# A decoder layer with every product turned to activations stationary, and its residual stream kept with tokens on the partitions

## The chip, the cores and the metric

The kernel runs on one core of one Trainium2 chip. The metric is the device time of one execution in microseconds (us). Names of engines: PE is TensorE (products and transposes), PEld its weight loads, DVE is VectorE, ACT is ScalarE, POOL is GpSimd, and SP's queue issues most DMAs.

## What is computed

One layer: two gated feed-forward blocks (SwiGLU) around a mixer of stick-breaking attention and a short convolution, each behind an RMS norm whose result is scaled and shifted by vectors (adaLN) that come from `c` through a 2048 x 18432 matrix. 256 tokens, width 2048, feed-forward width 5632, all float32.

```python
def swiglu(h, w_gu, w_down):
    gate, up = jnp.split(h @ w_gu, 2, axis=-1)
    return (jax.nn.silu(gate) * up) @ w_down
...
    mod = c_act @ w_ada[l] + b_ada[l]
    (sh1, sc1, g1, sh2, sc2, g2, sh3, sc3, g3) = jnp.split(mod, N_MOD, axis=-1)
    h = modulate(rms_norm(x), sh1, sc1)          # h * (1 + scale) + shift
    x = x + FFN_RES * g1[:, None, :] * swiglu(h, w1_gu[l], w1_down[l])
    h = modulate(rms_norm(x), sh2, sc2)
    x = x + g2[:, None, :] * hybrid_mixer(h, w_in[l], q_norm_w[l], k_norm_w[l], conv_w[l], w_out[l])
    h = modulate(rms_norm(x), sh3, sc3)
    x = x + FFN_RES * g3[:, None, :] * swiglu(h, w2_gu[l], w2_down[l])
```

In the mixer half of the width is attention (8 heads of 128), half is `gate_b * causal_short_conv(gate_c * u, conv_w)` with three taps along the tokens.

## The kernel before

**Weights and precision.** Each weight tile is 512 rows by 512 columns, one DMA of 1 MB on SP's queue into `raw` (five buffers). It is used in two halves of 256 rows. For each half ACT rounds the weights to the PE's fast float format (`high`, L358: `hi`) and DVE makes the rest (`prepare`, L364: `lo`). Activations are held the same way, as a pair of parts: `hS` for a normalised block, `act` and `mix` (tiles named `big`) for the inputs of the down and out products. A product is hi x hi + hi x lo + lo x hi.

**Two forms of product.** In `mm_N` (L477 to L486) the activations are stationary: for each of two groups of 128 tokens and each of two row blocks there are three products that stream 512 weight columns; the result has tokens on the partitions. In `mm_T` (L391) the weights are stationary: for each of four column blocks and two row blocks one product streams both parts of the activations (512 columns, L401) and one streams the high part (256 columns, L403); the result has channels on the partitions. `mm_D` (L406) splits the 512-column product in two of 256, used for the last column pair of a section. `mm_N` serves the gate and up columns and q, k, v; `mm_T` serves the down products, the convolution's c, u, b and the out products.

**Order of work.** `run` walks a list of entries written out by hand. For each half it emits `prepare`, then consumes the half that was prepared four halves earlier (AHEAD = 4): its products, and then `tick`, which emits work that was put off by a number of halves (`at`). In the last tile of a group the products of one pair of column blocks are held back (`held`) and follow in the last half, so the other pair finishes early. Each engine takes its instructions in the order in which they are emitted. Between weight tiles stand adaLN tiles (`ada_half`): DVE multiplies and adds them (L169), a block transpose and a sum fold them, and after some ticks (QP) one product of PE and four additions of DVE finish a section (L195, L203, L286).

**The start.** The first norm's scale and shift come in eight chunks of 256 channels (`ada_chunk`), mixed with weight tiles in eight windows (`windows`): two row blocks of `hS` become ready at each chunk's `end`, and column groups are visited several times, their partial sums being saved (L797) and loaded again (L776) by ACT. At a chunk's end all but two prepared halves are consumed (`keep`), then eight one-column products (`on_pe`, L233) finish the sums.

**The residual stream.** `xT` has channels on the partitions. x arrives with tokens on the partitions and is turned by 32 transposes (L598). `residual` copies the accumulator to `ev` on ACT (L463) and adds it on DVE with the gate as a value per partition (L638). The norm sums squares over partitions by products with ones (L672 to L677) and scales on DVE (L552); `norm_end` and `norm_rest` run in the gap between two sections (`fresh` in `run`). At the end `store` turns the result back (L842) and sends it from SP's queue.

Of the kernel before, what the change touches and what calls it, by code (L numbers as in the profile page):

```python
# [39 lines left out]
DB, DQ, DS, DL, DT = 1, 1, 0, 0, 0  # L40
OUT = 3
# [12 lines left out]
class Kern:  # L54
    def __init__(self, ctx, tc, x, c, w_ada, b_ada, w1_gu, w1_down, w_in, q_norm_w, k_norm_w,
                 conv_w, w_out, w2_gu, w2_down, out):
        self.tc, self.nc = tc, tc.nc
        self.x, self.c, self.out = x[0], c, out[0]
# [11 lines left out]
        self.ev = pool("ev", 2)  # L70
# [7 lines left out]
        self.have = set()  # L78

# [91 lines left out]
    def ada_half(self, sec, half):  # L171
# [25 lines left out]
        def finish():  # L197
            ps = st["ps"][:, 0:32].rearrange("p (j q) -> p q j", q=4)
            cs = slice(16 * sec + 8 * half, 16 * sec + 8 * half + 8)
            o, b = self.mod[:, cs], (self.b_lo[:, cs] if sec < 8 else self.b_hi[:, 8 * half:8 * half + 8])  # L200
            for q in range(4):
                r = slice(32 * q, 32 * q + 32)
                nc.vector.tensor_add(o[r], ps[r, q, :], b[r])  # L203
            self.ada_post(o, ("", "scale", "" if sec == 5 else "half")[sec % 3])
            self.have.add((sec, half))
# [19 lines left out]
    def ada_chunk(self, ch):  # L225
# [34 lines left out]
        def end():  # L260
            while self.soft:
                self.soft.popleft()()
# [7 lines left out]
            self.shifted(a, self.scaled(a))  # L270

        return ents, end

# [43 lines left out]
    def run(self, entries):  # L317
# [22 lines left out]
        for e in entries:  # L340
# [52 lines left out]
    def mm_T(self, accs, hi, lo, rhs, first, last, pairs=(0, 1)):  # L393

        nc = self.nc
        for pr in pairs:
            for i in range(2):
                for kk in range(2):
                    cs = slice((2 * pr + i) * P, (2 * pr + i + 1) * P)
                    o = accs[pr][i]  # L400
                    nc.tensor.matmul(o, hi[:, kk, cs], rhs[kk].rearrange("p a t -> p (a t)"),  # L401
                                     start=first and kk == 0, stop=False)
                    nc.tensor.matmul(o[:, 0:T], lo[:, kk, cs], rhs[kk][:, 0, :],  # L403
                                     start=False, stop=last and kk == 1)

    def mm_D(self, acc, hi, lo, rhs, first, last, i):  # L406

        nc = self.nc
        cs = slice((2 + i) * P, (3 + i) * P)
        o = acc[i][:, 0:T]  # L410
        for kk in range(2):
            nc.tensor.matmul(o, hi[:, kk, cs], rhs[kk][:, 0, :], start=first and kk == 0, stop=False)  # L412
            nc.tensor.matmul(o, hi[:, kk, cs], rhs[kk][:, 1, :], start=False, stop=False)  # L413
            nc.tensor.matmul(o, lo[:, kk, cs], rhs[kk][:, 0, :], start=False, stop=last and kk == 1)  # L414

    def group_T(self, w, rows, c0, rhs_of, finish, finish_one=None):
# [7 lines left out]
        def make(u):  # L424
            def cons(h, hi, lo):
                first, last = u == 0 and h == 0, u == nu - 1 and h == 1
                rhs = [rhs_of(4 * u + 2 * h + kk) for kk in range(2)]
                if first:
                    state["accs"] = [self.acc(), self.acc()]
                accs = state["accs"]  # L430
                if u < nu - 1 and finish_one:
                    self.mm_T(accs, hi, lo, rhs, first, False, (0,))
                    for i in range(2):
                        self.mm_D(accs[1], hi, lo, rhs, first, False, i)
                elif u < nu - 1:
                    self.mm_T(accs, hi, lo, rhs, first, False)
                elif h == 0:
                    self.mm_T(accs, hi, lo, rhs, first, False, (0,))
                    state["held"] = (accs, hi, lo, rhs, first, False, (1,))
                else:  # L440
                    self.mm_T(accs, hi, lo, rhs, False, True, (0,))
                    finish(0, accs[0])
                    if finish_one:
                        for i in range(2):
                            self.mm_D(accs[1], *state["held"][1:-1], i)
                            self.mm_D(accs[1], hi, lo, rhs, False, True, i)
                        for i in range(2):
                            finish_one(i, accs[1][i][:, 0:T])
                    else:
                        self.mm_T(*state["held"])  # L450
                        self.mm_T(accs, hi, lo, rhs, False, True, (1,))
                        finish(1, accs[1])
            return cons
# [5 lines left out]
    def evacuate(self, acc):  # L459

        c = self.ev.tile([P, 2, 512], F32, tag="ev", name=self.nm("ev"))
        for i in range(2):
            self.nc.scalar.copy(c[:, i, :], acc[i])  # L463
        return c

    def half_sum(self, acc, out):

        c = self.evacuate(acc)
        self.nc.vector.tensor_add(out, c[:, :, 0:T], c[:, :, T:2 * T])

    def split(self, dst, src):

        nc = self.nc
        nc.scalar.copy(dst[:, :, 0, :], src)  # L474
        nc.vector.tensor_sub(dst[:, :, 1, :], src, dst[:, :, 0, :].bitcast(F32))  # L475

    def mm_N(self, acc, hi, lo, h, first, last):  # L477

        nc = self.nc
        for tt in range(2):  # L480
            ts = slice(tt * P, (tt + 1) * P)
            for kk in range(2):
                nc.tensor.matmul(acc[tt], h[kk][:, 0, ts], hi[:, kk, :], start=first and kk == 0, stop=False, skip_group_check=True)  # L483
                nc.tensor.matmul(acc[tt], h[kk][:, 0, ts], lo[:, kk, :], start=False, stop=False, skip_group_check=True)  # L484
                nc.tensor.matmul(acc[tt], h[kk][:, 1, ts], hi[:, kk, :], start=False, stop=last and kk == 1,  # L485
                                 skip_group_check=True)  # L486

    def flip_split(self, dst, src):

        nc = self.nc  # L490
        for pr in range(2):
            ps = self.misc()
            for i in range(2):
                for tt in range(2):
                    nc.tensor.transpose(ps[:, i * T + tt * P:i * T + (tt + 1) * P],  # L495
                                        src[tt][:, (2 * pr + i) * P:(2 * pr + i + 1) * P], self.ident)
            self.split(dst[:, 2 * pr:2 * pr + 2], ps.rearrange("p (i t) -> p i t", i=2))
# [19 lines left out]
    def norm_end(self, sec):  # L517

        self.rrow = self.ssq
# [3 lines left out]
        s, y = self.tmp(), self.rrow  # L523
        v, t = s[:, 0:T], s[:, T:2 * T]
        nc.scalar.activation(y, self.ss[:, 0:T], AF.Ln, bias=self.epsb, scale=1.0 / D)
        nc.scalar.activation(y, y, AF.Exp, scale=-0.5)
        nc.scalar.activation(t, y, AF.Square)

        def norm_rest():
            for u in (sec, sec + 1):  # L530
                self.want(u, 0)
            nc.vector.tensor_scalar(v, self.ss[:, 0:T], 1.0 / D, EPS, op0=ALU.mult, op1=ALU.add)
            xn = self.tmp()[:, 0:512].rearrange("p (i t) -> p i t", i=2)
            sc = self.mod[:, 16 * (sec + 1):16 * (sec + 1) + 2]
            nc.vector.scalar_tensor_tensor(xn[:, 0, :], self.xT[:, 0, :], sc[:, 0:1], y, op0=ALU.mult, op1=ALU.mult)
            nc.vector.scalar_tensor_tensor(t, t, -0.5, v, op0=ALU.mult, op1=ALU.mult)
            nc.vector.scalar_tensor_tensor(xn[:, 0, :], t, 1.5, xn[:, 0, :], op0=ALU.add, op1=ALU.mult)
            nc.vector.scalar_tensor_tensor(y, t, 1.5, y, op0=ALU.add, op1=ALU.mult)
            nc.vector.scalar_tensor_tensor(xn[:, 1, :], self.xT[:, 1, :], sc[:, 1:2], y, op0=ALU.mult, op1=ALU.mult)
            self.shifted(0, xn)  # L540
            self.h_done = 2
            self.prepare(1)
            self.need_h(4)
        self.norm_rest = norm_rest

    def scaled(self, k):

        nc = self.nc
        xn = self.tmp()[:, 0:512].rearrange("p (i t) -> p i t", i=2)
        for i in range(2):  # L550
            sc = self.mod[:, 16 * (self.h_sec + 1) + k + i:16 * (self.h_sec + 1) + k + i + 1]
            nc.vector.scalar_tensor_tensor(xn[:, i, :], self.xT[:, k + i, :], sc, self.rrow, op0=ALU.mult, op1=ALU.mult)  # L552
        return xn

    def shifted(self, k, xn):

        nc = self.nc
# [571 lines left out]
```

## Time and profile before

| | before |
|---|---|
| median of 3 runs | 1926.17 us (1925.99 to 1926.94) |
| the profiled execution | 1926.24 us, span 1924.5 us |
| PE busy | 1894.2 us, 98% of the span |
| DVE busy | 1416.2 us, 74% |
| ACT busy | 941.1 us, 49% |
| DMA | 500.78 MB, mean 260 GB/s |

The profile is one execution. Busy time is what the recorded instructions cover; products of PE overlap in it, since their ends are modelled, so the distance between starts, not the duration, is what one of them costs. The granted clock is the share of full speed that PE was given; its two levels are 1.2 and 2.4 GHz (0.5 and 1.0). The chain is followed back from the last instruction to what released each step.

### The profile page before, as it was taken

To read this page: it belongs to the slowest core of one execution; us is meant where nothing else is said; L and a number is where in the kernel's file an instruction comes from. 1 tells how busy PE (TensorE), PEld (TensorE's weight loads), DVE (VectorE), ACT (ScalarE), POOL (GpSimd) and SP (SyncE) were. 2 spreads that over 40 slices of the span, in tenths; PEclk is the share of its full clock that TensorE was granted. 3 is DMA by queue.
4 is the path that set the end of the run, shared out by engine and by line. 5 is a ranking of instruction groups with operands and counts; after the bars stand their busy time and mean duration, and the time that the engine had idled before them with its cause. 6 is when DMAs were issued, how large, how long until landed. Compare 5 with 4: busy or idle time off the path is not lost.

```text
span 1924.5 us, 24141 instructions
## 1 busy us (share of the span) xinstructions
PE 1894.2 (98%) x9517; PEld 1606.1 (83%) x9517; DVE 1416.2 (74%) x1652; ACT 941.1 (49%) x1195; POOL 2.0 (0%) x11
## 2 busy tenths in 40 slices
PE   5999999999999999999999999999999999999999
PEld 4888888888888888788888887888888888888888
DVE  7878888788787889788889997667675554445454
ACT  4667784444444444466554554544444444444443
POOL 0000000000000000000000000000000000000000
PEclk8999999999999999999999999999999999999999
DMA  9898988888888878677869885678875555555551
GB/s 365 307 331 299 339 289 305 304 289 317 303 307 310 309 281 309 217 253 272 284 229 333 297 307 191 206 256 282 279 269 189 192 186 197 186 187 196 183 193 63
DMA packets 240361, 500.78 MB, mean 260 GB/s; under 512 B 8382, under 2 KB 43384, under 8 KB 239992
## 3 DMA queue, kind: packets, MB, share of 16 engines
q1 hardware_dynamic: 240216, 499.24, 74.0%
q8 instruction: 74, 1.21, 0.2%
q14 instruction: 39, 0.32, 0.0%
q10 hardware_dynamic: 32, 0.01, 0.0%
HBM read 497.12 MB, written 2.10 MB: 259 GB/s over the span
## 4 chain that ended last, share of the span: by engine, by line
PE 97%; DVE 2%; DMA 1%; ACT 0%; issue 0%; SPq 0%; DVEq 0%
PE acc L401 23%; PE acc L483 19%; PE acc L484 19%; PE acc L485 19%; PE acc L403 12%; DVE ada L169 1%; PE m L495 1%; PE acc L413 1%; PE acc L414 1%; DMA raw<-in_w_ada_dram 1%; PE acc L412 1%; DVE lo L364 0%; PE m L233 0%; PE m L1015 0%; PE m L992 0%
## 5 line engine op out<-in xcount | busy, mean ns | idle before, releaser
L364 DVE TENSOR_TENSOR lo<-raw,hi 128x1024 fp32r<-128x1024 f32 x656 | 792.7, 1223 | 392.4 <-ACT hi L358 389.5
L358 ACT CAST hi<-raw 128x1024 fp32r<-128x1024 f32 x656 | 685.9, 1053 | 737.4 <-PE acc L485 373.9
L483 PE MATMUL acc<-hi,hS 128*128 128x512 f32 x1600 | 632.1, 395 | 7.9 <-ACT hS L560 7.2
L484 PE MATMUL acc<-lo,hS 128*128 128x512 f32 x1600 | 627.7, 392 | 1.3 <-DVE lo L364 1.3
L485 PE MATMUL acc<-hi,hS 128*128 128x512 f32 x1600 | 627.4, 392 | 0.0
L401 PE MATMUL acc<-big,hi 128*128 128x512 f32 x1552 | 548.9, 398 | 0.0
L403 PE MATMUL acc<-big,lo 128*128 128x256 f32 x1552 | 436.4, 281 | 0.0
L169 DVE SCALAR_TENSOR_TENSOR ada<-raw,cact,ada 128x1024 f32<-128x1024 f32 (+1 forms) x327 | 357.2, 1092 | 8.3 <-DMA raw<-in_w_ada_dram 1.3
L483 PEld LDWEIGHTS acc<-hi,hS 128*128 128x128 f32 x1600 | 303.1, 189 | 70.7 <-ACT hS L560 8.1
L484 PEld LDWEIGHTS acc<-lo,hS 128*128 128x128 f32 x1600 | 303.0, 189 | 63.8 <-DVE lo L364 2.3
L485 PEld LDWEIGHTS acc<-hi,hS 128*128 128x128 f32 x1600 | 302.8, 189 | 64.0 <-DVE hS L563 0.6
L401 PEld LDWEIGHTS acc<-big,hi 128*128 128x128 f32 x1552 | 291.7, 188 | 68.3
L403 PEld LDWEIGHTS acc<-big,lo 128*128 128x128 f32 x1552 | 293.9, 189 | 0.2
L401 PE MATMUL acc<-hS,hi 128*128 128x512 f32 x384 | 136.5, 400 | 0.0
L403 PE MATMUL acc<-hS,lo 128*128 128x256 f32 x384 | 107.5, 280 | 0.0
L401 PEld LDWEIGHTS acc<-hS,hi 128*128 128x128 f32 x384 | 72.2, 188 | 16.8
L638 DVE SCALAR_TENSOR_TENSOR xT<-ev,mod,xT 128x256 f32<-128x256 f32 x148 | 60.9, 480 | 21.0 <-ACT ev L463 20.9
L403 PEld LDWEIGHTS acc<-hS,lo 128*128 128x128 f32 x384 | 72.5, 189 | 0.0
L463 ACT COPY ev<-acc 128x512 f32<-128x512 f32 x98 | 50.6, 593 | 29.6 <-PE acc L403 29.2
L797 ACT COPY big<-acc 128x512 f32<-128x512 f32 x72 | 41.0, 587 | 37.2 <-PE acc L485 37.2
L475 DVE TENSOR_TENSOR big<-m,big 128x512 fp32r<-128x512 f32 x44 | 28.4, 686 | 22.2 <-ACT big L474 22.1
L560 ACT ACTIVATE hS<-t,mod 128x256 fp32r<-128x256 f32 x48 | 22.0, 503 | 41.6 <-DVE t L552 39.0
(141 smaller groups left out, 710.6 us busy)
## 6 DMA issues: line engine op xcount, KB each, us to landing
raw<-in_w_gu_dram SPq DMA_DIRECT2D x170, 1024.0 KB, 5.4
raw<-in_w_ada_dram SPq DMA_DIRECT2D x112, 1024.0 KB, 5.1
raw<-in_w_down_dram SPq DMA_DIRECT2D x88, 1024.0 KB, 5.7
raw<-in_w_in_dram SPq DMA_DIRECT2D x48, 1024.0 KB, 6.4
raw<-in_w_ada_dram SPq DMA_DIRECT2D x64, 512.0 KB, 6.2
raw<-in_w_out_dram SPq DMA_DIRECT2D x16, 1024.0 KB, 6.4
raw<-in_w_gu_dram SPq DMA_DIRECT2D x12, 512.0 KB, 6.0
big<-in_x_dram SPq DMA_DIRECT2D x2, 1024.0 KB, 7.1
```

Source lines behind the costliest of these rows:

```text
L169: nc.vector.scalar_tensor_tensor(acc, w, self.cact[:, k:k + 1], acc, op0=ALU.mult, op1=ALU.add)
L358: nc.scalar.copy(hi, raw[:, 2 * h:2 * h + 2, :])
L364: nc.vector.tensor_sub(lo, raw[:, 2 * h:2 * h + 2, :], hi.bitcast(F32))
L401: nc.tensor.matmul(o, hi[:, kk, cs], rhs[kk].rearrange("p a t -> p (a t)"), start=first and kk == 0, stop=False)
L403: nc.tensor.matmul(o[:, 0:T], lo[:, kk, cs], rhs[kk][:, 0, :], start=False, stop=last and kk == 1)
L463: self.nc.scalar.copy(c[:, i, :], acc[i])
L475: nc.vector.tensor_sub(dst[:, :, 1, :], src, dst[:, :, 0, :].bitcast(F32))
L483: nc.tensor.matmul(acc[tt], h[kk][:, 0, ts], hi[:, kk, :], start=first and kk == 0, stop=False, skip_group_check=True)
L484: nc.tensor.matmul(acc[tt], h[kk][:, 0, ts], lo[:, kk, :], start=False, stop=False, skip_group_check=True)
L485: nc.tensor.matmul(acc[tt], h[kk][:, 1, ts], hi[:, kk, :], start=False, stop=last and kk == 1, skip_group_check=True)
L638: self.nc.vector.scalar_tensor_tensor(xd, src, self.mod[:, 16 * gate + d:16 * gate + d + 1], xd, op0=ALU.mult, op1=ALU.add)
L797: nc.scalar.copy(slot(n)[:, pr, :], acc[pr])
```

## The change

All products take the form of `mm_N`: `mm_T`, `mm_D` and `group_T` go, and `group_N` also serves down, c, u, b and out. x stays with tokens on the partitions (`x`, two tiles), so the residual adds along the free axis, with the gate as a row that is the same on all partitions: `gate_row` turns the gate's columns by one transpose, writes them to DRAM and reads them back broadcast, both on POOL's queue. The squares are summed along the free axis by ACT. A block is normalised in place of tokens (ACT, a factor per partition), turned by PE (`flip`) into PSUM, and scaled, shifted and split by DVE and ACT (`modulated`). The convolution's c x u and b are turned by `flip` too. The result is stored from `x` with no transposes. The `fresh` break in `run` goes, so tiles of the next section are prepared across the norm. In the list of adaLN sections (6, 0) and (7, 0) move ahead of (5, 0) and (5, 1). Cut to its core:

```diff
         def end():
+            xn = self.normed(CB * ch)
             while self.soft:
                 self.soft.popleft()()
...
-            self.shifted(a, self.scaled(a))
+            self.modulated(a, xn)
...
+    def gate_row(self, sec, half, cols):
+        nc = self.nc
+        ps = self.misc()
+        nc.tensor.transpose(ps[0:8, 0:P], cols, self.ident)
+        row = self.small.tile([8, P], F32, tag="row", name=self.nm("row"))
+        nc.scalar.copy(row, ps[0:8, 0:P])
+        flat = self.dram.tile([8, P], F32, tag="flat", name=self.nm("flat"))
+        nc.gpsimd.dma_start(flat, row)
+        g = self.gatep.tile([P, 1024], F32, tag="gate", name=self.nm("gate"))
+        nc.gpsimd.dma_start(g, flat.rearrange("j p -> (j p)").partition_broadcast(P))
+        self.gates[sec, half] = g
...
-            if e.get("fresh"):
-                self.high, self.prepare = high, prepare
-                while pend and pend[0][0] is not e["cons"]:
-                    consume()
-                self.norm_rest()
-                continue
...
+    def group_N(self, w, rows, c0, lhs_of, finish, lead=False):
...
             def cons(h, hi, lo):
+                k = 4 * u + 2 * h
+                first, last = k == 0, u == nu - 1
+                if lead:
+                    self.need_h(k + 2)
                 if first:
+                    state["acc"] = self.acc()
+                acc = state["acc"]
+                lhs = [lhs_of(k + kk) for kk in range(2)]
+                if not last:
+                    self.mm_N(acc, hi, lo, lhs, first, False)
                 elif h == 0:
+                    self.mm_N(acc, hi, lo, lhs, first, False, (0,))
+                    state["held"] = (hi, lo, lhs, first, False, (1,))
                 else:
+                    self.mm_N(acc, hi, lo, lhs, False, True, (0,))
+                    self.mm_N(acc, *state["held"])
+                    self.mm_N(acc, hi, lo, lhs, False, True, (1,))
+                if lead:
+                    self.need_h(k + 6)
+                if last and h == 1:
+                    finish(acc)
...
+    def normed(self, k):
+        xn = self.tmp()
+        for tt in range(2):
+            self.nc.scalar.activation(xn[:, tt * T:(tt + 1) * T], self.x[tt][:, k * P:(k + 2) * P], AF.Copy,
+                                      scale=self.r[:, tt:tt + 1])
+        return self.flip([xn[:, tt * T:(tt + 1) * T] for tt in range(2)])[0]
+
+    def modulated(self, k, xn):
+        nc = self.nc
+        h = self.tmp()[:, 0:512].rearrange("p (i t) -> p i t", i=2)
         for i in range(2):
+            sh, sc = (self.mod[:, 16 * sec + k + i:16 * sec + k + i + 1] for sec in (self.h_sec, self.h_sec + 1))
+            nc.vector.tensor_scalar(h[:, i, :], xn[:, i, :], sc, sh, op0=ALU.mult, op1=ALU.add)
+        nc.scalar.copy(self.hS[:, k:k + 2, 0, :], h)
+        nc.vector.tensor_sub(self.hS[:, k:k + 2, 1, :], h, self.hS[:, k:k + 2, 0, :].bitcast(F32))
...
+    def residual(self, dg, acc, gate):
+        nc = self.nc
+        self.want(gate, dg // 2)
+        g = self.gates[gate, dg // 2][:, 512 * (dg % 2):512 * (dg % 2 + 1)]
+        for tt in range(2):
+            t = self.tmp()[:, 0:512]
+            nc.vector.tensor_mul(t, acc[tt], g)
+            xd = self.x[tt][:, 512 * dg:512 * (dg + 1)]
+            nc.vector.tensor_add(xd, xd, t)
+
+    def squares(self, dg, next_sec):
...
+        for tt in range(2):
+            sq = self.tmp()[:, 0:512]
+            nc.scalar.activation(sq, self.x[tt][:, 512 * dg:512 * (dg + 1)], AF.Square,
+                                 accum_out=self.parts[:, tt, dg:dg + 1])
+        if dg == 3:
+            self.rms(self.parts)()
+            self.norm_begin(next_sec)
...
+    def store(self, dg):
+        for tt in range(2):
+            cs = slice(512 * dg, 512 * (dg + 1))
+            self.nc.sync.dma_start(self.out[tt * P:(tt + 1) * P, cs], self.x[tt][:, cs])
```

In the convolution `fin_u` multiplies the accumulator by c on DVE, and two ticks later flips the product; three passes of DVE per 128 channels then read it from PSUM. `fin_b` copies b on ACT and flips it two ticks later.

## Rows read from the trace of the kernel before

**Rows 1.** The page: busy us, share, instructions; the chain by engine.
```profile
PE 1894.2 (98%) x9517; PEld 1606.1 (83%) x9517; DVE 1416.2 (74%) x1652; ACT 941.1 (49%) x1195; POOL 2.0 (0%) x11
...
PE 97%; DVE 2%; DMA 1%; ACT 0%; issue 0%; SPq 0%; DVEq 0%
```

**Rows 2.** Stretches: us, busy us (count) per engine, granted clock, DMA share, GB/s.
```profile
100.00:150.00 50.00, 50.00 (x230) 41.64 (x229) 40.37 (x54) 35.54 (x54) 0.00 (x0) 1.00 0.87 311
```

**Rows 3.** Groups by line and shape: count, busy us, mean ns, idle before.
```profile
L401 PE MATMUL acc<-big,hi 128*128 128x512 f32 x1552 | 548.9, 398 | 0.0
...
L401 PE MATMUL acc<-hS,hi 128*128 128x512 f32 x384 | 136.5, 400 | 0.0
...
L412 PE MATMUL acc<-big,hi 128*128 128x256 f32 x112 | 31.7, 283 | 0.0
```

**Rows 4.** Chain in order of time (start, us, what), activations stationary, 32 pieces.
```profile
1649.97 0.23 PE acc L484
...
1657.00 0.23 PE acc L485
```

**Rows 5.** The same chain with weights stationary, 41 pieces.
```profile
1849.92 0.12 PE acc L403
...
1856.99 0.12 PE acc L403
```

**Rows 6.** The same chain: sums at the chunk ends (first, last of six), eight transposes.
```profile
78.56 0.79 PE m L233 x8
...
235.64 0.79 PE m L233 x8
258.36 0.87 PE m L495 x8
```

**Rows 7.** Timeline of ACT at the third chunk's end: start, us, line, idle before.
```profile
112.19 0.58 ACT L797 COPY big<-acc 128x512 f32<-128x512 f32 x1 [0.77 <-PE acc L485]
112.67 1.11 ACT L776 COPY acc<-big 128x512 f32<-128x512 f32 x2
```

**Rows 8.** Groups by line and shape, for durations of DVE and ACT.
```profile
L701 DVE TENSOR_TENSOR t<-acc,t 128x512 f32<-128x512 f32 x44 | 28.3, 684 | 0.2
...
L474 ACT CAST big<-m 128x512 fp32r<-128x512 f32 x44 | 23.7, 590 | 37.6 <-PE m L495 37.6
...
L846 DVE COPY t<-m 128x256 f32<-128x256 f32 x8 | 3.4, 425 | 6.5 <-PE m L842 6.5
...
L844 ACT COPY t<-m 128x256 f32<-128x256 f32 x8 | 3.0, 372 | 15.2 <-PE m L842 15.2
```

**Rows 9.** Timeline of the first norm: small operations of ACT and DVE.
```profile
14.77 0.28 ACT L503 ACTIVATE nr<-nt,epsb 128x2 f32<-128x2 f32 x1
...
17.46 0.16 DVE L507 TENSOR_SCALAR nt<-nt 128x2 f32<-128x2 f32 x1
```

**Rows 10.** Timeline of PE: a short stop, and the first boundary between sections.
```profile
37.64 0.50 PE L483 MATMUL acc<-hi,hS 128*128 128x512 f32 x1 [0.66 <-ACT big L797]
...
786.12 0.59 PE L672 MATMUL m<-ssq,ones 128*128 128x256 f32 x2
...
791.36 0.56 PE L483 MATMUL acc<-hi,hS 128*128 128x512 f32 x1 [2.92 <-ACT hS L560]
```

**Rows 11.** Stretches behind both boundaries and around the short stop.
```profile
791.36:796.00 4.64, 4.64 (x13) 3.48 (x14) 3.83 (x8) 2.65 (x5) 0.00 (x0) 0.63 0.15 15
1178.15:1185.00 6.85, 6.85 (x18) 5.38 (x19) 5.59 (x10) 4.87 (x7) 0.00 (x0) 0.56 0.39 124
36.00:42.00 6.00, 5.34 (x24) 4.09 (x23) 5.75 (x9) 5.01 (x8) 0.00 (x0) 1.00 1.07 392
```

**Rows 12.** Timeline of DVE and ACT where a gate's section is finished.
```profile
397.50 1.22 DVE L364 TENSOR_TENSOR lo<-raw,hi 128x1024 fp32r<-128x1024 f32 x1
...
397.84 1.05 ACT L358 CAST hi<-raw 128x1024 fp32r<-128x1024 f32 x1 [1.99 <-PE acc L401]
...
399.47 0.17 DVE L286 TENSOR_SCALAR mod<-mod 128x8 f32<-128x8 f32 x1
```

More of the change, by code (lines that the diff above doesn't have):

```diff
@@ L78, in __init__ @@
         self.have = set()
+        self.gates = {}
     def nm(self, s):
@@ L390, in run, with split, mm_N @@
         self.flush()
-    def mm_T(self, accs, hi, lo, rhs, first, last, pairs=(0, 1)):
+    def split(self, dst, src):
         nc = self.nc
[L396 to L406, printed above, removed]
-        nc = self.nc
[L409 to L416, printed above, removed]
+        nc.scalar.copy(dst[:, :, 0, :], src)
+        nc.vector.tensor_sub(dst[:, :, 1, :], src, dst[:, :, 0, :].bitcast(F32))
+    def mm_N(self, acc, hi, lo, h, first, last, tts=(0, 1)):
+        nc = self.nc
+        for tt in tts:
+            ts = slice(tt * P, (tt + 1) * P)
+            for kk in range(2):
+                nc.tensor.matmul(acc[tt], h[kk][:, 0, ts], hi[:, kk, :], start=first and kk == 0, stop=False,
+                                 skip_group_check=True)
+                nc.tensor.matmul(acc[tt], h[kk][:, 0, ts], lo[:, kk, :], start=False, stop=False, skip_group_check=True)
+                nc.tensor.matmul(acc[tt], h[kk][:, 1, ts], hi[:, kk, :], start=False, stop=last and kk == 1,
+                                 skip_group_check=True)
+    def group_N(self, w, rows, c0, lhs_of, finish, lead=False):
         state = {}
@@ L457, in group_T, with flip, flip_split @@
         return out
[L459 to L471, printed above, removed]
-        nc = self.nc
[L474 to L491, printed above, removed]
+    def flip(self, src):
+        nc = self.nc
+        out = []
+        for pr in range(src[0].shape[1] // T):
             ps = self.misc()
-            for i in range(2):
-                for tt in range(2):
+            for tt in range(2):
+                for i in range(2):
                     nc.tensor.transpose(ps[:, i * T + tt * P:i * T + (tt + 1) * P],
                                         src[tt][:, (2 * pr + i) * P:(2 * pr + i + 1) * P], self.ident)
-            self.split(dst[:, 2 * pr:2 * pr + 2], ps.rearrange("p (i t) -> p i t", i=2))
+            out.append(ps.rearrange("p (i t) -> p i t", i=2))
+        return out
+    def flip_split(self, dst, src):
+        for pr, ps in enumerate(self.flip(src)):
+            self.split(dst[:, 2 * pr:2 * pr + 2], ps)
     def rsqrt(self, y, v, x, scale, t):
@@ L515, in table, with norm_begin @@
         self.nc.scalar.preload_act_table_set("natural_log_exp_and_others")
-    def norm_end(self, sec):
-        self.rrow = self.ssq
+    def norm_begin(self, sec):
         self.hS = self.const.tile([P, KD, 2, T], F32R, tag="hS", name=self.nm("hS"))
         self.h_done, self.h_sec = 0, sec
-        nc = self.nc
[L523 to L544, printed above, removed]
@@ L627, in residual @@
[L627 to L640 removed]
+        self.norm_begin(0)
@@ L958, in conv, with copied @@
-            return (self.group_T(self.w_in, rows, 4 * AW + c, rhs, fin_c)
-                    + self.group_T(self.w_in, rows, 5 * AW + c, rhs, fin_u)
-                    + self.group_T(self.w_in, rows, 3 * AW + c, rhs, fin_b))
-        first = [self.group_N(self.w_in, c, f, c == 0) for c, f in
+            def copied(acc):
+                out = [self.tmp()[:, 0:512] for _ in range(2)]
+                for tt in range(2):
+                    nc.scalar.copy(out[tt], acc[tt])
+                return out
```

285 lines of the change are left out of this document (72 added, 213 removed).

## The prediction

> **What bounds the kernel now.** I read the page's busy shares and chain first, then the table of stretches, then the chain in order of time inside one stretch of each kind of product, and last the timeline around the few places where TensorE (PE) stands still. PE is busy 98% of the span and makes 97% of the chain that ended last [rows 1]; in 100 to 150 us it is never idle, at full granted clock, while VectorE (DVE) is busy 81%, ScalarE (ACT) 71% and the DMA engines 87% [rows 2]. So PE's own instructions, in their order, are the time: what leaves PE's stream is gained, what enters it or makes it wait is lost, and relief of DVE or ACT is worth nothing unless PE waits for it. PE takes its products in program order, and so do DVE and ACT; a PE instruction that waits holds every product behind it.
>
> **Products.** With activations stationary, one half tile of weights (256 rows, 512 columns) is 12 products of 512 columns. Between 1649.97 and 1657.00 lie 31 steps [rows 4]: 0.2268 us each, 2.72 us for 12. With weights stationary it is 8 pairs of 512 and 256 columns; 20 pairs take 7.07 us [rows 5]: 0.3535 us a pair, 2.83 us for 8. Both stream 6144 columns, so the gain is only that of 12 starts for 16. There are 1552 + 384 pairs and 112 triples of the split form [rows 3], which stand for a pair each: 2048, or 256 halves. The triples stand at the price of a pair. 256 x (2.828 - 2.721) = **-27.4 us**, all on PE and so all in the time.
>
> The Trainium skill ("TensorE: Matmul & The Clock Gate", "Back-to-back issue gap") gives a warm product N/2.4 + 2.5 ns. By that page, as an estimate, a pair is 325.0 ns and one and a half long products are 323.8 ns, so the gain would be 2.5 us in place of 27.4 and the time about 1976. The trace disagrees: each product costs more than its columns by over 10 ns, and the measurement decides.
>
> **Transposes.** Eight take 0.87 us [rows 6], 0.109 each. Added: three norms x 8 blocks x 4 = 96, of which the first 8 fall in the start, where PE idles; four flips of 8 in the convolution, 32; six for gates. Removed: seven of the eight stores, 28 (the last is in the tail). The 32 at the very start, taken out, lay beside loads: nothing. Net 88 + 32 + 6 - 28 = 98: **+10.7 us**.
>
> **Gates as rows.** A gate's transpose stands on PE right behind the half in whose tick DVE finishes the section, so PE waits for DVE. Today at 399.47 the last DVE step ends at 399.64, while the half ended by 397.84, when the next cast was released [rows 12]: 1.80 us late. The three others of its kind are 0.1, 0.5 and 1.5 late. Mean 1.0, six gates: **+6.0 us** (0 to 11). Their two transfers on POOL's queue have no row here; the sections are placed some tiles ahead of their first residual, so I take nothing, and price lateness under the rivals.
>
> **The six block ends at the start** (78.56 to 235.64, one at each group of the eight one-column products [rows 6]). At each, ACT saves the last visit's two banks and opens two others: these copies run from 112.19, when PE has just finished, to 113.78 [rows 7]. The new normalise passes of ACT come behind them and PE's four transposes behind these, and the transposes stand on PE ahead of the one-column products (`on_pe`) and of the two halves that `keep` holds back, so nothing of PE can run beside them. Two ACT passes of 128x256 at 0.37 [rows 8] end at 114.52, two last transposes 114.74: 2.55 us after PE ran dry, of which 0.44 stands under transposes. 6 x 2.1 = **+12.7 us**. The seventh end, at 47, is DVE's wait and hides it.
>
> The clock. A stop of 0.66 us left the granted clock at 1.00; after the gap at 791.36, behind 2.9 us of idle PE, it fell to the lower level: mean 0.63 over 4.64 us, 1.7 us lost; the other like it lost 0.44 x 6.85 = 3.0 us [rows 10, 11]. My stops of 2.5 us, in two pieces with light work, are nearer to the second kind. Bounds 0 and 6 x 3.0 = 18; I take the smaller loss at four of the six: **+6.9 us**.
>
> **The two norm boundaries.** Now, from the last down product (786.12) to the first product of the next section (791.36), 5.24 us [rows 10]; the second is like it. After, let t = 0 be the last product's end. The next cast waits for the held six products and starts 1.36 us before t; cast 1.05 and its low part 1.22 [rows 12] put DVE at the residual at 0.9. Multiply, add, twice, 4 x 0.684: 3.65. Square on ACT 0.59: 4.2. Four small DVE steps of 0.16 and two of ACT at 0.28 [rows 9]: 5.4. Two passes of ACT 0.74, two last transposes 0.22: 6.4. Two DVE passes 0.85, one of ACT 0.59 [rows 8]: 7.85. A dozen hand-overs of about 0.05 make 8.5 (8 to 10, if an adaLN step or two of DVE is queued ahead). So +3.3 each. Next, blocks 2 and 4 are flipped behind the first half: block 4's ACT passes wait for block 2's copy, that for DVE, that for the flip. PE, whose next product stands behind both flips, is idle for 0.85 + 0.59 + 0.74 = 2.2 us. Later blocks follow one per half; a cast (1.05) comes between, and I take 1.5 us in all (0 to 3). The clock: 3.0 us at each, against 1.7 and 3.0. Sum 2 x (3.3 + 2.2 + 1.5) + 1.3 - 0.8 (flips counted above) = **+14.5 us** (5 to 24). The column sums by ones that leave PE are inside the 5.24.
>
> **With one answer.** Residual from PSUM on DVE (four passes of 0.684 in place of eight short ones and ACT's copies) and the convolution's fewer sums: DVE and ACT are relieved, PE does not see it: 0; what hides them is PE's 2.72 us per half and the four halves prepared ahead, some 11 us. If that cover went, each would show. Gate 5 after sections 6 and 7: its first use is more than 20 tiles later: 0. Stores from x without transposes on SP's queue, ahead of the weight loads, as before: 0. The start loses two DVE scalings and a copy, the tail its transposes: 0, bounds -1.5 and +1. The flips of the convolution hold both small PSUM buffers while DVE reads six passes; attention's last steps and adaLN's sums want them: between 0 and 4 x 2.8; I take 1.5, since two ticks lie between.
>
> **Sum.** -27.4 + 10.7 + 6.0 + 12.7 + 6.9 + 14.5 + 1.5 = +24.9. The profiled execution is 1926.24 with 1924.5 of span, 0.07 above the median of the runs shown; 1926.2 + 24.9 = **1951 us**.
>
> **Rivals.** *Slower as summed* (1935 to 1970). *Covered flips:* ACT and DVE come to the flips before PE does, so that PE never waits; then only products and transposes count, with a little: 1926.2 - 27.4 + 10.7 = 1909.5, up to 1918. It decides where the normalise passes stand ahead of the saving copies or the next half already lies on PE. Against it: ACT's copies end 1.6 us after PE at a block end [rows 7], and the first blocks of a boundary form one chain. For it: DVE and ACT have idle time nearly everywhere. *A balance:* half of the stops and no clock falls: +24.9 - 6.9 - 14 = about +4, 1924 to 1930. *Gates arrive late:* a residual that waits for its row holds DVE and the low parts behind it; past the 11 us of prepared halves PE stands. Six gates, two or three late by some 8 us: 1970 to 1975. *The change does not give its gain:* products with activations stationary cost as much per column on the wide activation tiles as pairs do: 1951 + 27 = 1978. (The rule above leads to nearly the same.)
>
> **Chances.** As summed 0.68; covered flips 0.14; balance 0.08; late gates 0.07; no gain 0.03. A measurement of this kernel can tell about 0.2% (3.9 us) from no change. Faster: covered flips and the edge of the balance, 0.16; same 0.08; slower 0.76. Range 1918 to 1970: below it lies most of the covered case (0.12), above it most of the two dear ones (0.07); inside are the bounds of clock, gates and boundaries.
>
> **What would show it.** Right: products of 512 columns every 0.227 us where pairs stood; PE idle about 2 us before each of six flips below 240 us, released by ACT; 8 to 9 us between the sections and a second stop one half later; lower granted clock after these. Wrong: no PE idle time at the block ends, clock 1.00 through 50 to 250 us, or gate transposes that never wait. DVE's wait for a gate transfer would show the late gates.

## The result and the profile after

The changed kernel takes 1975.84 us (median of 4 runs, 1974.74 to 1977.97) against 1926.16 before: ratio 1.0258, 95% interval 1.0241 to 1.0276. That is 49.7 us slower, where 24.9 were forecast. The direction was right, the size was not, and the time lies above the range.

The page of the kernel after: busy time, and the chain that ended last by engine [rows 1 before].

```profile
PE 1897.0 (96%) x8429; PEld 1562.9 (79%) x8429; DVE 1385.0 (70%) x1508; ACT 905.9 (46%) x1130; POOL 8.6 (0%) x23
...
PE 91%; DVE 5%; ACT 2%; DMA 1%; issue 1%; SPq 0%; DVEq 0%; ACTq 0%
```

PE has 1088 instructions fewer and about the same busy time, but its part of the chain fell from 97% to 91%: DVE and ACT now make 7% of it. The waits of PE in the kernel after say where (what waited, for what; us in total, times, longest):

```profile
PE m L465 <- ACT t L502: 39.3, 17, 6.7
...
PE m L282 <- DVE mod L303: 6.1, 4, 3.1
PE acc L414 <- ACT hS L513: 5.5, 3, 2.0
...
PE m L282 <- DVE mod L204: 2.6, 1, 2.6
```

L465 are the transposes of a flip, L502 the normalise passes, L282 the transpose of a gate, L513 the copy that makes a block of `hS`. These are the three places that the forecast named: block ends and boundaries, and gates.

**Products.** The chain in order of time inside a steady stretch of the kernel after, in the second down group, where pairs stood before [rows 5]: 31 steps in 7.03 us, 0.2268 each, as [rows 4] had it.

```profile
1849.91 0.23 PE acc L417
...
1856.94 0.23 PE acc L414
```

**A block end at the start.** Timeline of ACT, then of PE, at the second of the six ends of the kernel after (start, us, line, idle before and releaser). It answers to [rows 7].

```profile
118.79 0.58 ACT L682 COPY big<-acc 128x512 f32<-128x512 f32 x1 [0.77 <-PE acc L417]
119.27 1.11 ACT L661 COPY acc<-big 128x512 f32<-128x512 f32 x2
120.31 0.91 ACT L502 ACTIVATE t<-x,nr 128x256 f32<-128x256 f32 x2
```
```profile
118.36 0.39 PE L417 MATMUL acc<-hi,hS 128*128 128x512 f32 x1
120.87 0.84 PE L465 MATMUL m<-ident,t 128*128 128x128 f32 x4 [2.12 <-ACT t L502]
121.55 0.95 PE L236 MATMUL m<-ones,ada 128*128 128x1 f32 x8
122.36 0.77 PE L414 MATMUL acc<-hi,hS 128*128 128x512 f32 x1
```

The passes stand behind the save and the loads of ACT, as forecast; PE waits 2.12 us for them. At all six ends PE is idle for 2.12 us: 12.7 in all (forecast 12.7). What follows is the surprise. Stretches of the kernel after around it (us, busy us and count of PE, PEld, DVE, ACT, POOL, granted clock, DMA share, GB/s):

```profile
122.00:124.00 2.00, 2.00 (x9) 1.71 (x9) 1.22 (x4) 0.18 (x1) 0.00 (x0) 0.59 0.00 0
124.00:126.00 2.00, 2.00 (x6) 1.56 (x6) 1.27 (x2) 2.00 (x3) 0.00 (x0) 0.55 0.00 0
126.00:128.00 2.00, 2.00 (x11) 1.64 (x10) 2.00 (x3) 2.00 (x3) 0.00 (x0) 1.00 0.00 0
```

PE is busy again from 120.87, but from 122 to 126 it gets about the lower clock. Behind five of the six ends it is so, for 4 to 8 us; behind the third, where PE starts again at 153.54, the clock stays at 1.00. The loss (busy time times what the granted clock lacks of 1.00, in stretches of 2 us) is 3.2, 1.7, 0, 3.4, 3.3 and 1.7 us at the six, 13.4 in all, against 6.9 forecast.

Which ends are followed by the lower clock is not fixed by the place. The traces of e3 and e4 below have the same program through the six ends and the same six stops of 2.12 us. In e3 the second, third, fourth and sixth fell (11.8 us lost), in e4 all but the fifth (13.4). The stretch behind the third end, first of the kernel after, then of e3:

```profile
151.00:158.00 7.00, 4.88 (x27) 3.76 (x26) 1.91 (x5) 3.94 (x8) 0.00 (x0) 1.00 0.59 216
```
```profile
152.00:158.80 6.80, 6.80 (x21) 5.79 (x22) 3.64 (x7) 3.32 (x4) 0.00 (x0) 0.50 0.01 5
```

**A boundary.** PE between the first two sections of the kernel after, and DVE in the same gap. It answers to [rows 10].

```profile
812.73 0.39 PE L417 MATMUL acc<-hi,big 128*128 128x512 f32 x1
819.80 1.11 PE L465 MATMUL m<-ident,t 128*128 128x128 f32 x4 [6.68 <-ACT t L502]
822.65 0.79 PE L414 MATMUL acc<-hi,hS 128*128 128x512 f32 x1 [1.74 <-ACT hS L513]
...
829.58 0.84 PE L465 MATMUL m<-ident,t 128*128 128x128 f32 x4 [2.15 <-ACT t L502]
```
```profile
812.88 1.23 DVE L381 TENSOR_TENSOR lo<-raw,hi 128x1024 fp32r<-128x1024 f32 x1 [0.34 <-ACT hi L375]
814.14 0.69 DVE L555 TENSOR_TENSOR t<-acc,gate 128x512 f32<-128x512 f32 x1
```

From the last product's start to the first of the next section it is 9.9 us, 9.7 from its end at 0.2268 (forecast 8.5), with a second stop of 2.15 (forecast 2.2). Part of the longer gap stands at its head: the residual begins behind the low part, 1.2 us after the product's end, where the forecast had 0.9.

**A gate.** The costliest of the six, on DVE and then on PE, kernel after [rows 12 before]:

```profile
1501.99 1.22 DVE L381 TENSOR_TENSOR lo<-raw,hi 128x1024 fp32r<-128x1024 f32 x1 [3.11 <-ACT hi L375]
1503.13 1.28 DVE L593 TENSOR_TENSOR t<-acc,t 128x512 f32<-128x512 f32 x2
...
1505.04 0.17 DVE L303 TENSOR_SCALAR mod<-mod 128x8 f32<-128x8 f32 x1
```
```profile
1505.36 0.37 PE L282 MATMUL m<-ident,mod 128*8 128x128 f32 x1 [3.14 <-DVE mod L303]
1505.38 0.77 PE L414 MATMUL acc<-hi,big 128*128 128x512 f32 x1
1505.96 0.63 PE L416 MATMUL acc<-lo,big 128*128 128x512 f32 x1
1506.38 0.63 PE L417 MATMUL acc<-hi,big 128*128 128x512 f32 x1
```

DVE has a low part and two multiplications of the SwiGLU (L593) in front of the section's end. The products behind start 0.42 us apart in place of 0.23: the clock has fallen here too.

### The profile page after: what moved, and what is told of

The parts are those of the page before. It is cut to its first block, busy times and chain, and to the rows that moved or that the text cites. A ratio compares the mean times of both kernels' runs of the same rounds, so it can differ in the third digit from the quotient of the medians.

```text
span 1974.2 us, 21656 instructions
## 1 busy us (share of the span) xinstructions
PE 1897.0 (96%) x8429; PEld 1562.9 (79%) x8429; DVE 1385.0 (70%) x1508; ACT 905.9 (46%) x1130; POOL 8.6 (0%) x23
## 3 DMA queue, kind: packets, MB, share of 16 engines
HBM read 500.27 MB, written 2.12 MB: 254 GB/s over the span
## 4 chain that ended last, share of the span: by engine, by line
PE 91%; DVE 5%; ACT 2%; DMA 1%; issue 1%; SPq 0%; DVEq 0%; ACTq 0%
PE acc L414 29%; PE acc L416 29%; PE acc L417 29%; PE m L465 2%; DVE lo L381 2%; DVE ada L170 1%; ACT hi L375 1%; DVE t L512 1%; PE m L236 0%; DMA raw<-in_w_ada_dram 0%; DMA raw<-in_w_gu_dram 0%; ACT t L502 0%; ACT acc L661 0%; SPq L347 0%; DVE x L557 0%
## 5 line engine op out<-in xcount | busy, mean ns | idle before, releaser
L414 PE MATMUL acc<-hi,hS 128*128 128x512 f32 x1792 | 714.3, 399 | 5.5 <-ACT hS L513 5.5
L416 PE MATMUL acc<-lo,hS 128*128 128x512 f32 x1792 | 706.2, 394 | 1.1 <-DVE lo L381 1.1
L417 PE MATMUL acc<-hi,hS 128*128 128x512 f32 x1792 | 705.5, 394 | 0.0
L414 PEld LDWEIGHTS acc<-hi,hS 128*128 128x128 f32 x1792 | 341.9, 191 | 75.4 <-ACT hS L513 6.4
L417 PEld LDWEIGHTS acc<-hi,hS 128*128 128x128 f32 x1792 | 341.4, 191 | 73.0 <-DVE hS L514 0.5
L416 PEld LDWEIGHTS acc<-lo,hS 128*128 128x128 f32 x1792 | 342.0, 191 | 70.7 <-DVE lo L381 1.6
L414 PE MATMUL acc<-hi,big 128*128 128x512 f32 x832 | 326.3, 392 | 0.0
L417 PE MATMUL acc<-hi,big 128*128 128x512 f32 x832 | 325.1, 391 | 0.0
L416 PE MATMUL acc<-lo,big 128*128 128x512 f32 x832 | 324.9, 391 | 0.0
L416 PEld LDWEIGHTS acc<-lo,big 128*128 128x128 f32 x832 | 157.0, 189 | 32.4
L417 PEld LDWEIGHTS acc<-hi,big 128*128 128x128 f32 x832 | 156.8, 189 | 32.6
L414 PEld LDWEIGHTS acc<-hi,big 128*128 128x128 f32 x832 | 157.0, 189 | 32.4
L465 PE MATMUL m<-ident,t 128*128 128x128 f32 x304 | 47.4, 288 | 41.3 <-ACT t L502 39.3
L465 PEld LDWEIGHTS m<-ident,t 128*128 128x128 f32 x304 | 35.4, 144 | 55.6 <-ACT t L502 48.6
L513 ACT CAST hS<-t 128x512 fp32r<-128x512 f32 x24 | 14.9, 620 | 66.5 <-DVE t L512 66.5
L661 ACT COPY acc<-big 128x512 f32<-128x512 f32 x72 | 40.0, 593 | 0.0
```

The costliest lines, as they stand in the source:

```text
L513: nc.scalar.copy(self.hS[:, k:k + 2, 0, :], h)
L661: nc.scalar.copy(st["acc", i][pr], slot(n)[:, pr, :])
```

## The experiments

**Theory** after seeing the result: the mechanisms are those of the forecast; the clock lost behind short stops and the gates' waits were priced too low. **Rivals:** the stops are filled by another wait once ACT is early; the stop itself, not the clock, is the loss; the products don't gain what the pitches say; gates that arrive late (the forecast's 1970 to 1975, near the measured time). The last one falls by the trace: the residual's multiplication waits for PE and not for a gate's transfer (kernel after, groups by line and shape):

```profile
L555 DVE TENSOR_TENSOR t<-acc,gate 128x512 f32<-128x512 f32 x40 | 27.4, 684 | 10.0 <-PE acc L417 9.9
```

**e1: normalise passes at the block ends one tile earlier.** `normed` is split; its ACT part, `scale_x`, is emitted before the products that the end consumes.

```diff
-... + [call(chunks[i + 1][1], keep=KEEP)]
+... + [call(lambda c=CB * (i + 1): k.scale_x(c), keep=AHEAD), call(chunks[i + 1][1], keep=KEEP)]
```

> The changed kernel (1975.8) with ACT's two normalise passes of each of the blocks 2 to 14 of the first norm emitted one tile earlier, ahead of the last visit's saving copies; the flips stay where they are. Theory A: the six stops of PE at the block ends (12.6 us idle) are the cause, and the low granted clock behind them (15.0 us lost) is their consequence: both go, 1975.8 - 27.6 = 1948. Rival B: the clock falls there because of the transposes and one-column products themselves, whether PE waits or not: only the idle time goes, 1963. Rival C: something else paces this stage (DVE, DMA), and PE waits for it a little later: under 6 us, 1970 to 1976.

Measured 1950.3 us (1.0126, 1.0111 to 1.0142): 25.5 us less. The stretch 50 to 272 us, first of the kernel after, then of e1:

```profile
50.00:272.00 222.00, 209.29 (x887) 171.06 (x888) 161.56 (x200) 142.36 (x206) 0.00 (x0) 0.93 0.78 277
```
```profile
50.00:272.00 222.00, 221.87 (x1019) 184.79 (x1020) 182.79 (x224) 161.15 (x237) 0.00 (x0) 0.99 0.89 318
```

PE's idle time goes from 12.7 to 0.1 us and the clock from 0.93 to 0.99, with no other change on PE. That is 12.6 of idle time and 13.4 of clock, 26.0 together: the place of two ACT instructions at each end was worth half of the loss. (The 15.0 us in the expectation includes 1.7 lost at 50 to 56 us, which are not behind these stops and which e1 keeps.) From 56 us on the clock is 1.00 in e1, though the same transposes and one-column products stand at the six ends: without the stop they did not lower it.

**e2: the stop kept, the clock held.** Nine products on old operands, whose result is not used, stand on PE ahead of each of the six flips; the flip still waits for ACT.

```diff
+            if ch > 1:
+                ps = self.misc()
+                for _ in range(9):
+                    nc.tensor.matmul(ps, self.hS[:, 0, 0, 0:P], self.hS[:, 0].rearrange("p a t -> p (a t)"), start=True, stop=True)
             xn = self.normed(CB * ch)
```

> The changed kernel with nine products of 512 columns (of hS with itself, into a small PSUM buffer that nobody reads) put on PE ahead of the flip at the six block ends: about 2.0 us of work in the 2.1 us in which PE now stands. Theory A: the stop costs nothing less, but the granted clock stays at its upper level: 15.0 us less, about 1961. Rival B (the clock falls for what comes behind, or for another reason): 1975 to 1977. If ACT were nearer than the trace says, the products would come on top: up to 6 x 2.0 = 12 us more, 1988.

Measured 1965.49 us (1961.22 to 1968.3; 1.0203, 1.0187 to 1.022): 10.4 us less, 14.6 in the run that was profiled. PE in e2 at the same block end, and its stretch:

```profile
118.52 0.48 PE L418 MATMUL acc<-hi,hS 128*128 128x512 f32 x1
118.83 0.39 PE L420 MATMUL acc<-lo,hS 128*128 128x512 f32 x1
119.06 0.40 PE L421 MATMUL acc<-hi,hS 128*128 128x512 f32 x1
```
```profile
50.00:272.00 222.00, 221.50 (x997) 181.65 (x996) 170.75 (x208) 150.86 (x220) 0.00 (x0) 0.99 0.82 294
```

The products behind the end start 0.31 and then 0.23 us apart. No useful work is done sooner in e2, so the gain is the clock alone: 10 to 15 us, where the stretches of after showed 13.4. That the stop alone is the loss falls.

**e3: the gate's row three halves later.**

```diff
-                self.gate_row(sec, half, o)
+                def row():
+                    self.gate_row(sec, half, o)
+                    self.have.add((sec, half))
+                self.at(2, row)
```

> The changed kernel with each gate's transpose (and its copy and its two transfers) emitted three halves later, when DVE has long finished the section. Theory A: PE's five waits there (8.7 us) and the low clock behind three of them (4.8 us) go: 1975.8 - 13.5 = 1962. Rival: the rows then arrive too late for the first residual, which holds DVE and with it PE: no gain, or a loss of some us a gate (1976 to 1990).

Measured 1961.89 us (1.019, 1.0173 to 1.0207): 13.9 us less. In the trace no transpose of a gate waits any more. The 8.7 us of waits and the 4.8 that the clock lost behind them in the trace of after make 13.5: the same size. The 4.8 is that of one execution. Behind the same stops, the traces of e1, e2 and e4 lost 3.0, 3.1 and 1.5 us.

**e4: normalise passes up to three blocks ahead, behind a boundary.**

```diff
                 if lead:
                     self.need_h(k + 2)
+                    self.ahead(k + 8)
```

> The changed kernel with ACT's normalise passes of the second and third norm emitted up to three blocks ahead of their flips, behind the copy of the block before the products of a half. Theory A: the second stop behind the first half of each section (2.15 and 0.35 or less) and the short ones behind later blocks (0.6 and 0.3 each) go, 6 to 7 us in all, and some of the low clock: 1966 to 1970. Rival: the passes only move the wait to the copy of the first block or to DVE's scaling of the next: 1974 to 1977. The first gap of each boundary (9.5 us) stays by both.

Measured 1968.38 us (1.0222, 1.0207 to 1.0237): 7.5 us less. The second stop of the first boundary, 2.15 us in the kernel after, is shorter in e4, and waits for the copy instead of the pass:

```profile
831.30 0.50 PE L415 MATMUL acc<-hi,hS 128*128 128x512 f32 x1 [1.30 <-ACT hS L521]
```

**e5: the three edits together.**

> The three edits of e1 (scaling passes of the chunk ends one tile earlier), e3 (gate rows three halves later) and e4 (passes up to three blocks ahead behind a boundary) together. Theory: the three terms are separate stops at separate places, so the gains of the single runs add: 1975.8 - 25.5 - 13.9 - 7.5 = 1929 us (1925 to 1932). What is left over the kernel before is then boundaries and transposes less products. Rival: the gains overlap, or a filled stop moves the wait to DVE or to the weight queue behind it; then 1936 or more.

Measured 1927.11 us (1.0011, 1.0001 to 1.0021, beside 1925.1 for the kernel before). One of its ten executions took 7409.23 us with the granted clock at 1.00; it is not in the ratio, no trace shows it, and its cause is open. The gains add, within 2 us. What is left is next to nothing over the kernel before.

**e6: a shorter chain in the boundary.** At a section's end the last half is consumed before the next one is prepared, and the next norm's first block is emitted ahead of the next cast.

```diff
             for h in range(2):
+                if len(pend) == AHEAD and pend[0][1] == 1 and pend[0][0] in self.finals:
+                    consume()
                 prepare(h)
...
             self.norm_begin(next_sec)
+            self.need_h(2)
```

> e5, and at a section's end the last half is consumed before the next half is prepared (so that DVE's residual does not stand behind a low part), and the first block of the next norm is emitted right behind the sums of squares on ACT, ahead of the next cast. Theory: each boundary is one chain of DVE and ACT that begins when PE ends; the low part of 0.9 us at its head and the cast of 1.0 us in its middle go, about 3 us for both boundaries with the clock as it is: 3 to 4 us under e5 (about 1925). Rival: the preparation that is put off is late afterwards and PE waits for it, so nothing is gained, or the loss of the clock keeps the time within 1 us of e5.

Measured 1922.89 us (0.9989, 0.998 to 0.9998): 4.2 us under e5. PE's wait for the first flip, 6.68 in the kernel after, is 4.90 in e6, but the products behind still run at half speed:

```profile
786.13 1.11 PE L474 MATMUL m<-ident,t 128*128 128x128 f32 x4 [4.90 <-ACT t L517]
788.98 0.79 PE L422 MATMUL acc<-hi,hS 128*128 128x512 f32 x1 [1.74 <-ACT hS L528]
789.57 0.63 PE L424 MATMUL acc<-lo,hS 128*128 128x512 f32 x1
790.00 0.63 PE L425 MATMUL acc<-hi,hS 128*128 128x512 f32 x1
```

**e7: the gap filled.** e6, with dummy products in both gaps.

```diff
+            ps = self.misc()
+            for _ in range(19):
+                nc.tensor.matmul(ps, self.hS[:, 0, 0, 0:P], self.hS[:, 0].rearrange("p a t -> p (a t)"), start=True, stop=True)
             self.norm_begin(next_sec)
             self.need_h(2)
+            ps = self.misc()
+            for _ in range(4):
+                nc.tensor.matmul(ps[:, 0:T], self.ones, self.x[0][:, 0:T], start=True, stop=True)
```

> e6, and 19 dummy products of 512 columns (old operands, result unused) on PE in each boundary's gap ahead of the first flip, and four of 256 columns in float32 behind it. Theory: the gap is a chain of DVE and ACT of 8 to 9 us in which PE has nothing to do, so products put there cost nothing, and the transposes and products behind the gap run at the higher clock: about 1.1 us for the transposes and 2 us behind, at each of two boundaries, 4 to 6 us under e6 (about 1920). Rival: PE is the bound here too and the dummies come on top: 19 x 0.227 + 4 x 0.3 = 5.5 us at each boundary, 11 us over e6.

Measured 1919.52 us (1916.78 to 1920.35; 0.9969, 0.9958 to 0.9981): 3.4 us under e6, and 0.3% faster than the kernel before. In e7 the first products behind the gap start 0.33 to 0.39 us apart and soon 0.23, and the granted clock of the whole execution is 0.999, against 0.995 in e6:

```profile
787.03 0.50 PE L422 MATMUL acc<-hi,hS 128*128 128x512 f32 x1
787.36 0.40 PE L424 MATMUL acc<-lo,hS 128*128 128x512 f32 x1
787.75 0.50 PE L425 MATMUL acc<-hi,hS 128*128 128x512 f32 x1
788.09 0.39 PE L422 MATMUL acc<-hi,hS 128*128 128x512 f32 x1
788.31 0.39 PE L424 MATMUL acc<-lo,hS 128*128 128x512 f32 x1
```

**e8: the price of a start.** e5, with 1040 products of the second feed-forward block's down part split in two halves of 256 columns.

```diff
+        cs = [slice(0, 256), slice(256, 512)] if self.halve else [slice(0, 512)]
...
-                nc.tensor.matmul(acc[tt], h[kk][:, 0, ts], lo[:, kk, :], start=False, stop=False, skip_group_check=True)
+                for c in cs:
+                    nc.tensor.matmul(acc[tt][:, c], h[kk][:, 0, ts], lo[:, kk, c], start=False, stop=False,
+                                     skip_group_check=True)
```

> e5, with the products of the second feed-forward block's down part split in two of 256 columns (88 halves x 12 products, less 16 that open an accumulator: 1040 products more, the columns the same). It measures the term on which the forecast of -27.4 us rests, the price of a product's start. Theory: from rows 4 and 5 a start costs 0.0135 us (columns at 2.4 a ns) to 0.0266 us (both rows solved for a column and a start), so 1040 x that = 14 to 28 us over e5. Rival: a start costs next to nothing and the gain of the change came from something else in its form; then within 3 us of e5. Third: a load of the stationary side isn't hidden behind 256 columns; then well over 28 us. By the Trainium skill (TensorE: Matmul & The Clock Gate, Back-to-back issue gap) a start costs 2.5 ns, as an estimate 2.6 us for all.

Measured 1940.82 us (1.0083, 1.0068 to 1.0098): 13.7 us over e5, 0.0132 a start. The chain in e8 shows 60 pieces of two products in 14.40 us, 0.1200 a product:

```profile
1880.10 0.24 PE acc L422 x2
...
1894.50 0.24 PE acc L422 x2
```

The Trainium skill ("TensorE: Matmul & The Clock Gate", "Back-to-back issue gap") gives 2.5 ns over the columns for an isolated warm product. This run shows 13.2 ns in a stream, and the measurement decides. But 0.2268 + 0.1200 is 0.3468 and not the 0.3535 of a pair [rows 5]. So only half of what a pair cost over one and a half long products is starts: 0.0066 of 0.0133 us.

**b0: the kernel before, profiled once more.** In its trace pairs had two prices: over 72 pairs in each 25 us the mean was 0.3467 in the first down group of the second feed-forward block (1475 to 1575 us), and near 0.3535 in most other stretches where pairs stand.

> The kernel before, profiled once more, to see whether the two prices of a pair of 512 and 256 columns come back: 0.3467 us in the first down group of the second feed-forward block, 0.3535 us in all other groups. If the price is a matter of the group (place of its operands, order of the work), the same group is cheap again and the others are not; if it is a matter of the execution, the cheap stretch moves, grows or is gone. The time of the whole: 1926 us.

Measured 1924.84 us (one run). Chain in b0, 22 pairs in the cheap group (7.62 us, 0.3464 each) and 22 in the next down group (7.78, 0.3536):

```profile
1510.05 0.23 PE acc L401
...
1517.67 0.23 PE acc L401
```
```profile
1847.92 0.24 PE acc L401
...
1855.70 0.23 PE acc L401
```

The price belongs to the place in the program, then, not to the execution. It is a mean: in both traces single pairs of the dear groups take 0.350 or 0.361 us, about two to one, and those of the cheap group 0.346 or 0.347. A short stretch in the mixer, 1008 to 1024 us, is as cheap in both (0.3467), so the expectation's "all other groups" was too strong. In the cheap group the price is just the sum of the two products of e8. What sets it I have not found: traffic (190 and 191 GB/s) and busy shares of DVE and ACT are alike in both groups. It stays open.

**e9: the price of transposes.** e5, each transpose of the new flips issued twice.

```diff
-            for tt in range(2):
+            for tt in [0, 1] * times:
```

> e5, and each transpose of the new flips issued a second time (96 of the three norms and 32 of the convolution, 128 in all; the flips of the feed-forward activations, which the kernel before has too, stay single). It measures the term of +10.7 us. Theory: each costs 0.109 us on PE, in the boundary gaps up to twice that: 128 x 0.109 = 14 us, less the first 4 in the start, plus 8 x 0.1 in the gaps: 13 to 15 us over e5. Rival: transposes hide in the waits they stand behind, or cost more because each pulls the clock down: under 8 or over 20 us.

Measured 1942.07 us (1.0082, 1.0065 to 1.0099): 13.7 us over e5 by the two ratios, 15.0 by the medians, so 0.107 to 0.117 for each of 128. The price from [rows 6] holds.

## Why the forecast was right in direction and wrong in size

| term | forecast | measured | by |
|---|---|---|---|
| products | -27.4 | -24.7 | 208 halves x 0.1067 and 48 x 0.0523 |
| transposes | +10.7 | +10.5 to 11.5 | 98 x 0.107 to 0.117, e9 |
| gates, waits | +6.0 | +8.7 | waits after; e3 13.9 with the next |
| gates, clock | 0 | +4.8 | stretches after; 1.5 to 3.1 in e1, e2, e4 |
| block ends, waits | +12.7 | +12.7 | idle time, 50 to 272 us |
| block ends, clock | +6.9 | +13.4 | stretches; e2 10 to 15; both e1 25.5 |
| boundaries | +14.5 | about +17 | delay at equal work, less flips |
| convolution, start, rest | +1.5 | +2.4 | waits after; before had 1.0 of its own |
| sum | +24.9 | about +45 | of +49.7 |

The delay at equal work is the time at which both kernels have streamed the same number of columns, kernel after less kernel before. It grows by 30.3 us over the six block ends (27.6 without their transposes, of which the rows name 26.1), by 11.7 and 11.6 at the boundaries (24 with the products' gain in them put back, less 7.0 for flips), and falls by 0.86 in each eight halves of most down groups. Some 4 to 5 us are not in the table; two or three of them lie in the mixer, where groups gained 0.2 to 0.3 in place of 0.86. Another part is how idle time is counted, from the modelled end of a product (0.39 us behind its start) and not from where the next could have started (0.23): by an estimate 0.16 us at each of eleven stops, 1.8 in all.

**Right.** What bounds the kernel; that ACT's passes come behind the saving copies and PE stands 2.1 us at six places (by starts of products 2.3, from 118.59 to 120.87, so the exact 12.7 is partly luck: the two passes took 0.91 us in place of 0.74); the boundary as one chain of DVE and ACT, with the second stop of 2.2 us; the transposes; that the start, the tail and the gates' transfers cost next to nothing. The rival of covered flips is false for this change, by the very reason that was given against it.

**Wrong: the clock.** The step that failed is "I take the smaller loss at four of the six". The two rows at hand, a stop of 0.66 us and a gap with 2.9 us of idle PE [rows 10, 11], left the case between them open, and I took a value below the middle of 0 to 18. The trace of after shows five of six falling, at 1.7 to 3.4 us each: 13.4. The upper bound covers this; the choice inside the bounds was the error: the count was nearly right, the price was not, 2.7 us on average where 1.7 was taken, with three ends above the dearer row. For the gates I wrote no clock term at all, though three of their six stops are as long as 1.9 to 3.1 us. In the trace of after the clock at these two kinds of place is 11.3 of the 24.8 us by which the forecast fell short; since the falls differ between executions (11.8 and 13.4 at the ends in e3 and e4, 1.5 to 4.8 at the gates), this is good to 3 us or so.

**Wrong: the gates' waits**, 8.7 for 6.0. I took the mean lateness of four sections of the kernel before; which steps stand ahead on DVE differs by place, and at 1505 us it was two long multiplications beside the low part. That the bound of 11 held is little comfort.

**Wrong: the products**, by 2.7. One stretch of pairs [rows 5] stood for all 256 halves, and 48 of them were cheaper. The triples of the split form, taken at the price of a pair, cost 0.3596 us, which works the other way, by 0.7 in all. The boundaries were 2 to 3 us too low, a part of it the low part of DVE ahead of the residual, the read-back of 0.19 us behind each pass of squares, which the forecast left out, and the cast that stands on ACT ahead of the normalise passes (e6 moved the first and the last, for 4.2 us).

**The time alone misleads.** 1975.8 us is near what two other rivals gave, the late gates (1970 to 1975) and products without gain (1978). Neither took place: no residual waits for a gate's transfer, and products start 0.2268 us apart. Only the trace parts them from three terms that were all mis-sized in one direction.

## What to carry to other kernels

Where one engine is the bound, a step that a change places at that engine's head of queue is worth what stands ahead of its producer in the producer's queue: moving two ACT passes one tile forward at each of six block ends gave back 25.5 us, and with three such moves the change was level with the kernel before. Price a stop of TensorE with the clock behind it, which cost here as much as the stop, and look for three kinds of place: ends of blocks, boundaries, and small products that turn the result of another engine. Where a stop can't be removed, products on old data in it can hold the clock (3 to 15 us here), and a forecast by bounds should say why it takes the lower one.

## What was not expected of the hardware

- A stop of about 2 us can be followed by a spell at the lower clock: 13.4 us over five of six stops of 2.12 us, each followed by four transposes and eight one-column products. Neither the length of the stop nor its place decided. The six stops of the same program lost 11.8 us behind four of them in e3 and 13.4 behind five in e4, not the same ones. The stop of 2.15 us at 829.58 left the clock at 1.00, its twin at the second boundary did not (below). At the gates the stops of 1.91, 2.64 and 3.14 us were followed by the lower clock in the kernel after, those of 0.72 us and less were not (1.00 over 1401 to 1405 us, around that of 0.72); in e1, e2 and e4 a stop of 1.92 or 1.93 at the first of these places was not. What tells them apart is open. A stretch of the kernel after around the stop of 1.91, and the second boundary's second stop with the stretch behind it:

```profile
427.00:433.00 6.00, 4.77 (x15) 3.78 (x16) 2.32 (x7) 1.55 (x3) 0.52 (x1) 0.72 1.04 391
```
```profile
1231.21 1.05 PE L465 MATMUL m<-ident,t 128*128 128x128 f32 x4 [2.15 <-ACT t L502]
```
```profile
1231.70:1235.10 3.40, 3.40 (x11) 2.82 (x12) 1.86 (x4) 1.77 (x3) 0.00 (x0) 0.50 0.00 0
```

- Nine products on old data in a stop of 2.1 us held the clock at 1.00 (e2).
- A start of a product costs 13.2 ns over its columns (e8), and a pair of 512 and 256 columns with weights stationary costs 0.3467 or 0.3535 us on average by its place in the program, the same in two executions.
